# The interleaved MLP stages of a decoder trunk: from the scheduler's order to an order written in the source

## The chip, the cores and the metric

One core of a Trainium2 chip runs the whole program. The metric is the device time of one execution in microseconds (us). The engines are TensorE (PE in the profile; its weight loads are PEld), VectorE (DVE), ScalarE (ACT), GpSimd (POOL) and SyncE (SP), which issues the weight transfers.

## The reference

A trunk of two layers over 256 tokens of width 2048, in float32. Each layer is a mixer (MLA beside mLSTM in the first, dilated window attention in the second) and then an MLP; a final norm follows. The change touches the MLPs alone:

```python
def squared_relu_mlp(h, w1, w2):
    return jnp.square(jax.nn.relu(h @ w1)) @ w2     # w1: 2048 x 8192, w2: 8192 x 2048

x = x + squared_relu_mlp(rms_norm(x, norm_mlp[layer]), mlp_w1[layer], mlp_w2[layer])
```

## The kernel before, in words

**Splitting.** Every weight tile comes by one 512 KB transfer on SP's queue into one of four raw buffers (`load`, L118) and is split into two float32r halves (`halves`, L130): ScalarE copies it to "hi" (L135), then VectorE subtracts to get "lo" (L136). Four hi and four lo buffers serve the ordinary splits. A product is three matmuls: hi by hi, hi by lo, lo by hi (`mm_three`, L152).

**First matrix.** The hidden width of 8192 is done in four quarters (NQ) of 16 blocks of 128 columns. A block (`blocks`, L1089, by `steps_feats`, L265) takes two weight tiles; for each, `mm_feats` (L158) issues 8 matmuls of 512 columns (L164, operands T and wh) and 8 of 256 (L168, wl). It accumulates in the PSUM bank of `acc(..., 3)`, L95: each of the four "acc" banks is one buffer. After the second tile `evac_h` (L1031) empties it: ScalarE copies it out (bt_h, L1037), VectorE adds the two halves (hu, L1039), ScalarE applies ReLU and the square. For two blocks at a time of the first 12 of a quarter (SEVEN = 6 pairs), VectorE then forms differences in hp (L1053 to L1055) and the result pt is split (L1057, L1058); each of the last four blocks is split as it is (ht, L301 and L302).

**Second matrix.** Per quarter and per half of the output columns (c = 0 and 1024), `steps_seven` (L193) does 6 pairs of block rows by a seven-product scheme and the last two pairs plainly. A pair has two steps. `go_a` loads two raw tiles r0 and r1, forms the sums ta and tb on VectorE (L224 to L226), splits r0, half of r1, ta and tb, and issues three products (9 matmuls) into the "ym" tiles m1, m5, m7. `go_b` issues four products (12 matmuls): one into m6, three into the accumulators "yc" in banks 0, 1 and 2, in the order (1,0), (0,1), (0,0). The four ym tiles take the other four PSUM banks. A plain step (`eight`, L248) has one weight tile and 12 matmuls into yc; the second of them opens the fourth accumulator (1,1) in bank 3.

**Emptying.** After the last pair `early_y` (L1063) uses m1, m5, m6, m7: one ScalarE copy and eight VectorE operations, four of which add into x (L1067). After the last plain step `late_y` (L1082) adds the four yc tiles into x (L1086), in the order (1,1), (1,0), (0,1), (0,0).

**Order.** A stage is one quarter's half of the output columns, interleaved with the 8 blocks of the first matrix that are next: with c = 0 blocks 8 to 15 of the same quarter, with c = 1024 blocks 0 to 7 of the next. `woven` (L444) puts one or two steps of the pairs ahead of each block: a b block, a block, b a block, b block, and so on, with a block last; then come the four plain steps. A layer has seven such stages, then a last part on its own. Within the order that the source gives, the framework's scheduler decides at compile time how the instructions stand in each engine's queue. Each queue is worked through in its order.

Of the kernel before, what the change touches and what calls it, by code (L numbers as in the profile page):

```python
# [14 lines left out]
P = 128  # L15
# [54 lines left out]
def trunk(ctx: ExitStack, tc: tile.TileContext, plan, a, c_first, c_even, c_odd, out):  # L70
# [122 lines left out]
    def steps_seven(pool, H, pairs, w, c, early, late, name="y", hold=()):  # L193
# [12 lines left out]
        def seven(k):  # L206
            first, last = k == pairs[0], k == pairs[-1]
            end = last and not rest
            t = {}

            def product(ac, i, h, l, j, last):
                pt = H[2 * k][0]
                mm_three(ac, (pt[:, 0, i, :], pt[:, 1, i, :]), (h[:, j, :], l[:, j, :]), first, last)

            def go_a():
                if first:
                    box["m"] = {i: mis(f"{name}m{i}") for i in (1, 5, 7, 6)}
# [43 lines left out]
            return go  # L261

        return [seven(k) for k in pairs], [[eight(k, j) for j in range(2)] for k in rest]

    def steps_feats(Ts, w, c0, evac, n=256, name="f", kt=4, bank=None):  # L265

# [757 lines left out]
    def mlp(layer, norm, nxt):  # L1024
        st = ExitStack()
        sm = st.enter_context(tc.tile_pool(name=f"mlp{layer}", bufs=1))
        X = Late(norm.T)
        scale = {}
        NF = FF // NQ // P

        def evac_h(H):  # L1031
            def make(c):
                box = {}

                def go(f, ac):
                    t = sm.tile([P, 512], F32, name="bt_h", tag="bt", bufs=2)
                    nc.scalar.activation(t, ac, AF.Copy)  # L1037
                    u = sm.tile([P, S], F32, name="hu", tag="hu", bufs=2)
                    nc.vector.tensor_add(u, t[:, :S], t[:, S:])  # L1039
                    nc.scalar.activation(u, u, AF.Relu)  # L1040
                    if c >= SEVEN:
                        nc.scalar.activation(u, u, AF.Square)
                        H[2 * c + f] = sm.tile([P, 2, S], FR, name="ht", tag="ht", bufs=2 * (NF // 2 - SEVEN))
                        split_to(H[2 * c + f], u)
# [5 lines left out]
                    v = u.rearrange("p (b t) -> p b t", b=NB)  # L1050
                    nc.scalar.activation(dst, v, AF.Square)
                    if f == 1:
                        nc.vector.tensor_tensor(r[:, 4:6, :], r[:, 1:3, :], r[:, 2:4, :], OP.subtract)  # L1053
                        nc.vector.tensor_tensor(r[:, 6, :], r[:, 5, :], r[:, 1, :], OP.subtract)
                        nc.vector.tensor_tensor(r[:, 7, :], r[:, 0, :], r[:, 6, :], OP.add)  # L1055
                        pt = sm.tile([P, 2, 8, P], FR, name="pt", tag="pt", bufs=SEVEN)
                        nc.scalar.activation(pt[:, 0], r, AF.Copy)  # L1057
                        nc.vector.tensor_tensor(pt[:, 1], r, pt[:, 0].bitcast(F32), OP.subtract)  # L1058
                        H[2 * c], H[2 * c + 1] = (pt, 0), (pt, 1)
                return go  # L1060
            return make

        def early_y(c):  # L1063
            def go(m1, m5, m6, m7):
                def add(b, j, src):
                    v = x[b][c + j]
                    nc.vector.scalar_tensor_tensor(v, src, scale["s"][:, b:b + 1], v, OP.mult, OP.add)  # L1067

                p = sm.tile([P, 512], F32, name="yp", tag="yp", bufs=1)
                q = sm.tile([P, 512], F32, name="yq", tag="yq", bufs=1)  # L1070
                nc.scalar.activation(p, m1, AF.Copy)
                add(0, 0, m1)
                nc.vector.tensor_add(p, m6, p)
                nc.vector.tensor_add(q, m7, p)
                nc.vector.tensor_sub(p, m5, p)
                add(1, 0, q)
                nc.vector.tensor_sub(q, m5, q)
                add(0, 1, p)
                add(1, 1, q)
            return go  # L1080

        def late_y(c):  # L1082
            def go(cc):
                for b, j in ((1, 1), (1, 0), (0, 1), (0, 0)):
                    v = x[b][c + j]
                    nc.vector.scalar_tensor_tensor(v, cc[b, j], scale["s"][:, b:b + 1], v, OP.mult, OP.add)  # L1086
            return go

        def blocks(q, H):  # L1089

            ev = evac_h(H)

            def block(i):
                def go():
                    run(steps_feats(X, ("mlp_w1", layer, 0), q * (FF // NQ) + i * P,
                                    lambda f, ac: ev[i // 2](i % 2, ac), n=P, name="h", kt=8, bank=3))
                return go

            ev = [ev(c) for c in range(NF // 2)]
            return [block(i) for i in range(NF)], ev  # L1100

        H = [None] * NF
        hs, ev = blocks(0, H)
        steps = steps_feats(X, ("mlp_w1", layer, 0), 0, ev[0], name="h")
        run(steps[:3])
        norm.turn(3)
        run(steps[3:])
        norm.close()
        scale["s"] = norm.inv_var()
        for c in range(1, NF // 4):  # L1110
            run(steps_feats(X, ("mlp_w1", layer, 0), c * 256, ev[c], name="h"))
        for q in range(NQ):
            last = q == NQ - 1
            wq = ("mlp_w2", layer, q * (FF // NQ))
            seven, eight = steps_seven(sm, H, list(range(SEVEN)), wq, 0, early_y(0), late_y(0))
            woven(hs[NF // 2:], sum(seven, []))
            run(*eight)
            if last and nxt is None:
                finish(H, wq, early_y(2), scale, sm)
                break  # L1120
            pairs = list(range(3 if last else SEVEN))
            seven, eight = steps_seven(sm, H, pairs, wq, 1024, early_y(2), late_y(2))
            if last:
                nxt.stats(0)
                nxt.stats(1)
                steps = sum([a + b for a, b in zip(seven, eight)] + eight[len(seven):], [])
                run(steps[:-1], [lambda: nxt.turn(0)], steps[-1:], [lambda: nxt.turn(1)])
                break
            H = [None] * NF
            hs, _ = blocks(q + 1, H)  # L1130
            sv = sum(seven, [])
            woven(hs[:NF // 2], sv)
            run(*eight)
        if nxt is not None:
            nxt.stats(2)
            nxt.stats(3)
        return st
# [63 lines left out]
```

## Time and profile before

| | us |
|---|---|
| runs (3), median | 2117.52 |
| lowest, highest | 2115.13, 2119.45 |
| profiled execution, its time | 2115.02 |
| profiled execution, its span | 2113.2 |

The span is from the first to the last instruction in the trace. In rows of a timeline the first number is the start in us, the second the duration; ends of matmuls are modelled, so how long one takes in a sequence is read from start to start. "Idle before" names what the engine waited for.

### The profile page before, as it was taken

To read this page: it belongs to the slowest core of one execution; us is meant where nothing else is said; L and a number is where in the kernel's file an instruction comes from. 1 tells how busy PE (TensorE), PEld (TensorE's weight loads), DVE (VectorE), ACT (ScalarE), POOL (GpSimd) and SP (SyncE) were. 2 spreads that over 40 slices of the span, in tenths; PEclk is the share of its full clock that TensorE was granted. 3 is DMA by queue.
4 is the path that set the end of the run, shared out by engine and by line. 5 is a ranking of instruction groups with operands and counts; after the bars stand their busy time and mean duration, and the time that the engine had idled before them with its cause. 6 is when DMAs were issued, how large, how long until landed. Compare 5 with 4: busy or idle time off the path is not lost.

```text
span 2113.2 us, 29343 instructions
## 1 busy us (share of the span) xinstructions
PE 2093.8 (99%) x10860; PEld 1797.8 (85%) x10860; DVE 1742.3 (82%) x2455; ACT 1303.7 (62%) x1876; POOL 6.1 (0%) x13
## 2 busy tenths in 40 slices
PE   9999999999999999999999999999999999999998
PEld 8998888888888888888888888888888888888886
DVE  5678555889999999999877667568899998999998
ACT  6575445766676666667544444457666666667665
POOL 0000000000000000000000000000000000000000
PEclk9999999999999999999999999999999999999999
DMA  8554455556565566566665555455565665656664
GB/s 295 165 174 158 160 176 187 178 191 216 183 211 197 190 202 204 192 205 195 197 194 174 170 179 170 163 186 178 193 205 194 206 201 188 204 194 200 203 213 162
DMA packets 115296, 404.51 MB, mean 191 GB/s; under 512 B 12944, under 2 KB 13584, under 8 KB 115152
## 3 DMA queue, kind: packets, MB, share of 16 engines
q1 hardware_dynamic: 114048, 400.02, 57.9%
q8 instruction: 85, 1.39, 0.3%
q0 software_dynamic: 384, 1.51, 0.2%
q10 hardware_dynamic: 720, 1.11, 0.1%
q14 instruction: 59, 0.48, 0.1%
HBM read 400.49 MB, written 2.10 MB: 191 GB/s over the span
## 4 chain that ended last, share of the span: by engine, by line
PE 88%; DVE 7%; DMA 2%; issue 1%; ACT 1%; SPq 0%; POOLq 0%; POOL 0%; DVEq 0%; ACTq 0%
PE h L164 21%; PE h L168 11%; PE yc L155 4%; PE yc L156 4%; PE yc L154 4%; PE ym L155 4%; PE ym L156 3%; PE ym L154 3%; DVE wl L136 3%; PE k L164 3%; PE o L154 3%; PE o L156 3%; PE o L155 3%; PE q L164 3%; PE v L154 2%; PE v L156 2%
## 5 line engine op out<-in xcount | busy, mean ns | idle before, releaser
L136 DVE TENSOR_TENSOR wl<-wr,wh 128x1024 fp32r<-128x1024 f32 (+4 forms) x769 | 865.6, 1134 | 259.8 <-ACT wh L135 254.5
L135 ACT ACTIVATE wh<-wr 128x1024 fp32r<-128x1024 f32 (+4 forms) x769 | 753.8, 986 | 515.6 <-PE h L164 136.6
L164 PE MATMUL h<-T,wh 128*128 128x512 f32 x2048 | 511.4, 392 | 1.1 <-ACT wh L135 0.9
L164 PEld LDWEIGHTS h<-T,wh 128*128 128x128 f32 x2048 | 374.5, 188 | 76.0 <-ACT wh L135 2.6
L168 PEld LDWEIGHTS h<-T,wl 128*128 128x128 f32 x2048 | 279.3, 190 | 20.1
L168 PE MATMUL h<-T,wl 128*128 128x256 f32 x2048 | 285.5, 282 | 0.0
L155 PE MATMUL ym<-wl,pt 128*128 128x512 f32 x360 | 142.2, 395 | 1.8 <-DVE wl L136 1.8
L154 PE MATMUL ym<-wh,pt 128*128 128x512 f32 x360 | 140.1, 394 | 0.2 <-ACT wh L135 0.2
L156 PE MATMUL ym<-wh,pt 128*128 128x512 f32 x360 | 140.2, 389 | 0.0
L224 DVE TENSOR_TENSOR ta<-wr,wr 128x1024 f32<-128x1024 f32 x90 | 110.1, 1223 | 33.1 <-DMA wr<-in_mlp_w 32.4
L135 ACT ACTIVATE wh<-ta 128x1024 fp32r<-128x1024 f32 x90 | 95.2, 1058 | 61.0 <-DVE ta L224 60.9
L155 PE MATMUL yc<-wl,pt 128*128 128x512 f32 x318 | 124.0, 390 | 0.0
L154 PE MATMUL yc<-wh,pt 128*128 128x512 f32 x318 | 123.2, 390 | 0.0
L156 PE MATMUL yc<-wh,pt 128*128 128x512 f32 x318 | 122.8, 389 | 0.0
L1040 ACT ACTIVATE hu<-hu 128x256 f32<-128x256 f32 x128 | 52.6, 415 | 99.5 <-DVE hu L1039 99.3
L135 ACT ACTIVATE wh<-tb 128x1024 fp32r<-128x1024 f32 x90 | 94.7, 1052 | 28.5 <-DVE tb L226 28.3
L136 DVE TENSOR_TENSOR wl<-tb,wh 128x1024 fp32r<-128x1024 f32 x90 | 109.7, 1219 | 1.9 <-ACT wh L135 1.7
L136 DVE TENSOR_TENSOR wl<-ta,wh 128x1024 fp32r<-128x1024 f32 x90 | 109.7, 1219 | 0.0
L154 PE MATMUL o<-wh,M 128*128 128x512 f32 x256 | 102.3, 399 | 0.0
L156 PE MATMUL o<-wh,M 128*128 128x512 f32 x256 | 99.8, 390 | 0.0
L155 PE MATMUL o<-wl,M 128*128 128x512 f32 x256 | 99.7, 389 | 0.0
L154 PE MATMUL yc<-wh,ht 128*128 128x512 f32 (+1 forms) x256 | 99.4, 388 | 0.0
(297 smaller groups left out, 3320.9 us busy)
## 6 DMA issues: line engine op xcount, KB each, us to landing
wr<-in_mlp_w SPq DMA_DIRECT2D x512, 512.0 KB, 4.1
wr<-in_od_w_qkv SPq DMA_DIRECT2D x96, 512.0 KB, 4.1
wr<-in_ev_w_in SPq DMA_DIRECT2D x32, 512.0 KB, 3.5
wr<-in_ev_w_out SPq DMA_DIRECT2D x32, 512.0 KB, 3.4
wr<-in_od_w_out SPq DMA_DIRECT2D x32, 512.0 KB, 3.5
wr<-in_ev_w_in SPq DMA_DIRECT2D x24, 344.0 KB, 3.1
wr<-in_ev_w_in SPq DMA_DIRECT2D x15, 364.0 KB, 5.8
wr<-in_mla_w_ukv SPq DMA_DIRECT2D x8, 512.0 KB, 3.7
```

Source lines behind the costliest of these rows:

```text
L135: nc.scalar.activation(hi, raw, AF.Copy)
L136: nc.vector.tensor_tensor(lo, raw, hi.bitcast(F32), OP.subtract)
L154: nc.tensor.matmul(ac, xh, hi, start=first, stop=False)
L155: nc.tensor.matmul(ac, xh, lo, start=False, stop=False)
L156: nc.tensor.matmul(ac, xl, hi, start=False, stop=last)
L164: nc.tensor.matmul(acs[f], hi[:, j, f * P:(f + 1) * P], Ts[j].rearrange("p a t -> p (a t)"), start=first and j == 0, stop=False)
L168: nc.tensor.matmul(acs[f][:, :S], lo[:, j, f * P:(f + 1) * P], Ts[j][:, 0, :], start=False, stop=last and j == n - 1)
L224: nc.vector.tensor_tensor(ta, r0, r1[:, 0:1, :].to_broadcast([P, 2, 512]), OP.add)
L1040: nc.scalar.activation(u, u, AF.Relu)
```

## The change

`drive` takes a list of units and writes out, for ScalarE, VectorE and TensorE, the very order in which they work (`manual_schedule`). A unit has its splits and sums (`prep`), its matmuls (`go`) and the kinds of buffers that it frees. At step n, `drive` first emits what is due "now", then splits for coming units, as far as buffers of the kinds w (4), t (3) and q (1) are left, alternating with the other work that is due; the first split that finds no buffer stops those behind it. Then come unit n's matmuls. What these return (copies, additions) is due one to four units later. Each stage's order is the pattern, with "s" for a pair (two units) and "h" for a block (two units), and then the four plain units. All 14 stages are in two such lists, one per layer. The half tile of r1 gets buffers of its own (q); ta has one buffer instead of two; the late additions come as (1,0), (0,1), (0,0), (1,1).

```diff
-                ta = pool.tile([P, 2, 512], F32, name=f"ta{n_w[0]}", tag="ta", bufs=2)
+                ta = pool.tile([P, 2, 512], F32, name=f"ta{n_w[0]}", tag="ta", bufs=1)
...
+    def drive(units, left):
+        ahead = [(n, kind, f) for n, u in enumerate(units) for kind, f in u.prep]
+        due = {}
+        for n, u in enumerate(units):
+            first, rest = due.pop(n, ([], []))
+            splits = []
+            while ahead and left.get(ahead[0][1], 1) > 0:
+                _, kind, f = ahead.pop(0)
+                if kind:
+                    left[kind] -= 1
+                splits.append(f)
+            assert not ahead or ahead[0][0] > n
+            run(first, [f for pair in zip(splits, rest) for f in pair], splits[len(rest):], rest[len(splits):])
+            for d, now, f in u.go() or ():
+                due.setdefault(n + d, ([], []))[not now].append(f)
+            for kind in u.free:
+                left[kind] += 1
...
+            return [Unit([(None, sums), ("w", split(0, lambda: t["r0"])), ("t", split(1, lambda: t["ta"], pool, "t", 3))],
+                         go_a, ["t"]),
+                    Unit([("q", split(3, lambda: t["r1"][:, 1:2, :], pool, "q", 1)),
+                          ("t", split(2, lambda: t["tb"], pool, "t", 3))], go_b, ["w", "q", "t"])]
...
+                due = [(1, True, copy), (1, False, add), (2, False, square)]
+                if c >= SEVEN:
+                    return due + [(3, False, plain)]
+                return due + ([(3, False, sums), (4, False, pair)] if f == 1 else [])
...
+                return [(1, True, both(nc.scalar.activation, p, m1, AF.Copy)),
+                        (1, True, add(0, 0, m1)),
+                        (1, False, both(nc.vector.tensor_add, p, m6, p)),
+                        (1, False, both(nc.vector.tensor_add, q, m7, p)),
+                        (2, False, both(nc.vector.tensor_sub, p, m5, p)),
+                        (2, False, add(1, 0, q)),
+                        (3, False, both(nc.vector.tensor_sub, q, m5, q)),
+                        (3, False, add(0, 1, p)),
+                        (4, False, add(1, 1, q))]
...
+                return [(1, True, add(b, j)) for b, j in ((1, 0), (0, 1), (0, 0), (1, 1))]
...
+                    if g == 0:
+                        box["a"] = acc("h", 3)
+                    mm_feats([box["a"]], [X[k] for k in range(8 * g, 8 * g + 8)], *t["w"], g == 0, g == 1)
+                    if g == 1:
+                        return ev(i, box["a"])
...
+        pattern = "shshhshhshhshs"
+        units = []
         for q in range(NQ):
...
+                for what in pattern:
+                    units += (seven if what == "s" else hs).pop(0)
+                units += eight
...
+        with tc.manual_schedule(engines={mybir.EngineType.PE, mybir.EngineType.Activation, mybir.EngineType.DVE}):
+            drive(units, {"w": 4, "t": 3, "q": 1})
```

## Rows read from the trace of the kernel before

**Rows 1.** The page, part 1: busy time of each engine over the span.

```profile
PE 2093.8 (99%) x10860; PEld 1797.8 (85%) x10860; DVE 1742.3 (82%) x2455; ACT 1303.7 (62%) x1876; POOL 6.1 (0%) x13
```

**Rows 2.** Busy times by stretch, the interleaved parts; columns PE, PEld, DVE, ACT, POOL, clock, DMA.

```profile
400.00:1000.00 600.00, 598.42 (x3048) 509.22 (x3047) 558.25 (x680) 400.80 (x537) 0.00 (x0) 1.00 0.61 198
1470.00:2050.00 580.00, 578.43 (x2948) 491.12 (x2947) 537.97 (x658) 387.21 (x515) 1.12 (x2) 1.00 0.61 199
```

**Rows 3.** The timeline of TensorE, one block of the first matrix: start, duration.

```profile
407.20 1.98 PE L164 MATMUL h<-T,wh 128*128 128x512 f32 x8
409.01 1.11 PE L168 MATMUL h<-T,wl 128*128 128x256 f32 x8
409.96 2.00 PE L164 MATMUL h<-T,wh 128*128 128x512 f32 x8
411.81 1.12 PE L168 MATMUL h<-T,wl 128*128 128x256 f32 x8
412.76 0.40 PE L154 MATMUL ym<-wh,pt 128*128 128x512 f32 x1
```

**Rows 4.** Groups of TensorE's matmuls between 400 and 1000 us: count, busy, mean.

```profile
L164 PE MATMUL h<-T,wh 128*128 128x512 f32 x904 | 225.0, 391 | 0.5 <-ACT wh L135 0.5
L168 PE MATMUL h<-T,wl 128*128 128x256 f32 x904 | 126.0, 282 | 0.0
```

**Rows 5.** The timeline at the end of a block: two matmuls in flow, the next unit, the copy.

```profile
606.68 0.62 PE L164 MATMUL h<-T,wh 128*128 128x512 f32 x2
...
608.09 0.40 PE L154 MATMUL ym<-wh,pt 128*128 128x512 f32 x1
...
608.30 0.58 ACT L1037 ACTIVATE bt_h<-h 128x512 f32<-128x512 f32 x1
```

**Rows 6.** The timeline where TensorE waited for a block's copy.

```profile
1820.90 0.58 ACT L1037 ACTIVATE bt_h<-h 128x512 f32<-128x512 f32 x1
...
1821.53 0.73 PE L164 MATMUL h<-T,wh 128*128 128x512 f32 x2 [0.15 <-ACT bt_h L1037]
```

**Rows 7.** The timeline of VectorE in the plain steps at a stage's end.

```profile
480.88 1.23 DVE L224 TENSOR_TENSOR ta<-wr,wr 128x1024 f32<-128x1024 f32 x1
482.02 0.69 DVE L136 TENSOR_TENSOR wl<-wr,wh 128x512 fp32r<-128x512 f32 x1
482.62 0.69 DVE L225 TENSOR_TENSOR tb<-ta,wr 128x512 f32<-128x512 f32 x1
483.23 1.23 DVE L136 TENSOR_TENSOR wl<-ta,wh 128x1024 fp32r<-128x1024 f32 x1
484.37 1.41 DVE L1086 SCALAR_TENSOR_TENSOR x<-yc,iv_mlp,x 128x512 f32<-128x512 f32 x2
485.69 0.68 DVE L226 TENSOR_TENSOR tb<-tb,wr 128x512 f32<-128x512 f32 x1
```

**Rows 8.** Groups of ScalarE between 400 and 1000 us: the split's first half.

```profile
L135 ACT ACTIVATE wh<-wr 128x1024 fp32r<-128x1024 f32 x185 | 194.3, 1055 | 83.3 <-PE h L164 57.8 <-PE yc L156 13.2 <-issue 7.4
```

**Rows 9.** Busy times from 470 to 504 us, across a stage's end; columns as above.

```profile
470.00:504.00 34.00, 34.00 (x172) 28.92 (x171) 33.58 (x41) 21.04 (x28) 0.00 (x0) 1.00 0.58 201
```

**Rows 10.** VectorE's waits between 400 and 1000 us: total, times, longest.

```profile
DVE ta L224 <- DMA wr<-in_mlp_w: 13.0, 18, 1.6
```

**Rows 11.** Busy times of the last 9 us; columns as above.

```profile
2104.00:2113.00 9.00, 0.95 (x8) 0.75 (x7) 3.31 (x11) 2.78 (x8) 0.56 (x1) 0.66 0.55 202
```

**Rows 12.** The timeline of TensorE at the start of the program.

```profile
4.44 0.98 PE L154 MATMUL c<-wh,T 128*128 128x364 f32 x2 [4.44 <-ACT wh L135]
...
10.35 0.51 PE L155 MATMUL c<-wl,T 128*128 128x364 f32 x1
10.65 0.51 PE L156 MATMUL c<-wh,T 128*128 128x364 f32 x1
...
11.22 0.33 PE L155 MATMUL c<-wl,T 128*128 128x364 f32 x1
11.39 0.33 PE L156 MATMUL c<-wh,T 128*128 128x364 f32 x1
```

More of the change, by code (lines that the diff above doesn't have):

```diff
@@ new lines, in units_seven, with seven, product, sums @@
+    def units_seven(pool, H, pairs, w, c, early, late, name="y"):
+        box = {}
+        rest = [k for k in range(len(H) // 2) if k not in pairs]
+        def seven(k):
+            first, last = k == pairs[0], k == pairs[-1]
+            t = {}
+            def product(ac, i, h, l, j, last):
+                pt = H[2 * k][0]
+                mm_three(ac, (pt[:, 0, i, :], pt[:, 1, i, :]), (h[:, j, :], l[:, j, :]), first, last)
+            def sums():
+                t["r0"] = r0 = load(w, [(2 * k, c, 512), (2 * k + 1, c + 512, 512)], (2, 512))
+                t["r1"] = r1 = load(w, [(2 * k, c + 512, 512), (2 * k + 1, c, 512)], (2, 512))
+                n_w[0] += 1
+                t["ta"] = ta = pool.tile([P, 2, 512], F32, name=f"ta{n_w[0]}", tag="ta", bufs=1)
+                t["tb"] = tb = pool.tile([P, 2, 512], F32, name=f"tb{n_w[0]}", tag="tb", bufs=1)
+                nc.vector.tensor_tensor(ta, r0, r1[:, 0:1, :].to_broadcast([P, 2, 512]), OP.add)
+                nc.vector.tensor_tensor(tb[:, 0, :], ta[:, 0, :], r0[:, 1, :], OP.add)
+                nc.vector.tensor_tensor(tb[:, 1, :], tb[:, 0, :], r1[:, 1, :], OP.add)
+            def split(to, src, *where):
+                def go():
+                    t[to] = halves(src(), *where)
+                return go
+            def go_a():
+                if first:
+                    box["m"] = {i: mis(f"{name}m{i}") for i in (1, 5, 7, 6)}
+                m = box["m"]
+                product(m[1], 1, *t[0], 0, last)
+                product(m[5], 5, *t[1], 0, last)
+                product(m[7], 4, *t[1], 1, last)
+            def go_b():
+                if first:
+                    box["c"] = {i: acc(f"{name}c{i[0]}{i[1]}", n) for n, i in enumerate(((1, 0), (0, 1), (0, 0)))}
+                m, cc = box["m"], box["c"]
+                end = last and not rest
+                product(m[6], 6, *t[2], 0, last)
+                product(cc[1, 0], 3, *t[2], 1, end)
+                product(cc[0, 1], 7, *t[0], 1, end)
+                product(cc[0, 0], 0, *t[3], 0, end)
+                if last:
+                    return early(m[1], m[5], m[6], m[7])
+            return [Unit([(None, sums), ("w", split(0, lambda: t["r0"])), ("t", split(1, lambda: t["ta"], pool, "t", 3))],
+                         go_a, ["t"]),
+                    Unit([("q", split(3, lambda: t["r1"][:, 1:2, :], pool, "q", 1)),
+                          ("t", split(2, lambda: t["tb"], pool, "t", 3))], go_b, ["w", "q", "t"])]
+        def eight(k, j):
+            t = {}
+            def split():
+                t["w"] = weights(w, 2 * k, 2, c + 512 * j, 512)
+            def go():
+                cc = box["c"]
+                if k == rest[0] and j == 1:
+                    cc[1, 1] = acc(f"{name}c11", 3)
+                hi, lo = t["w"]
+                for i in range(2):
+                    for b in range(NB):
+                        mm_three(cc[b, j], operand(H[2 * k + i], b), (hi[:, i, :], lo[:, i, :]),
+                                 (b, j) == (1, 1) and k == rest[0] and i == 0, k == rest[-1] and i == 1)
+                if k == rest[-1] and j == 1:
+                    return late(cc)
+            return Unit([("w", split)], go, ["w"])
+        return [seven(k) for k in pairs], [eight(k, j) for k in rest for j in range(2)]
@@ L1091, in blocks, with at_once, units_h, unit @@
+            return due
+        def at_once(f):
+            return lambda *arg: run([go for _, _, go in f(*arg)])
+        w1 = ("mlp_w1", layer, 0)
+        def units_h(q, H, blocks):
             ev = evac_h(H)
-            def block(i):
+            def unit(i, g, box):
+                t = {}
+                def split():
+                    t["w"] = weights(w1, 8 * g, 8, q * (FF // NQ) + i * P, P)
                 def go():
-                    run(steps_feats(X, ("mlp_w1", layer, 0), q * (FF // NQ) + i * P,
-                                    lambda f, ac: ev[i // 2](i % 2, ac), n=P, name="h", kt=8, bank=3))
-                return go
@@ L1099, in blocks @@
-            ev = [ev(c) for c in range(NF // 2)]
-            return [block(i) for i in range(NF)], ev
+                    if g == 0:
[3 more added lines that the diff above has]
+                        return ev(i, box["a"])
+                return Unit([("w", split)], go, ["w"])
+            out = []
+            for i in blocks:
+                box = {}
+                out.append([unit(i, g, box) for g in range(2)])
@@ L1102, in mlp, with evac @@
+            return out
         H = [None] * NF
-        hs, ev = blocks(0, H)
-        steps = steps_feats(X, ("mlp_w1", layer, 0), 0, ev[0], name="h")
+        ev = evac_h(H)
+        def evac(c):
+            return lambda f, ac: run([go for _, _, go in ev(2 * c + f, ac)])
+        steps = steps_feats(X, w1, 0, evac(0), name="h")
         run(steps[:3])
@@ L1110, in mlp @@
         for c in range(1, NF // 4):
-            run(steps_feats(X, ("mlp_w1", layer, 0), c * 256, ev[c], name="h"))
+            run(steps_feats(X, w1, c * 256, evac(c), name="h"))
+        pattern = "shshhshhshhshs"
+        units = []
         for q in range(NQ):
-            last = q == NQ - 1
             wq = ("mlp_w2", layer, q * (FF // NQ))
-            seven, eight = steps_seven(sm, H, list(range(SEVEN)), wq, 0, early_y(0), late_y(0))
-            woven(hs[NF // 2:], sum(seven, []))
-            run(*eight)
@@ L1118, in mlp @@
[L1118 to L1133, printed above, removed]
+            G = [None] * NF
+            for c, hs in ((0, units_h(q, H, range(NF // 2, NF))), (1024, units_h(q + 1, G, range(NF // 2)))):
+                if q == NQ - 1 and c > 0:
+                    break
+                seven, eight = units_seven(sm, H, list(range(SEVEN)), wq, c, early_y(c // 512), late_y(c // 512))
+                for what in pattern:
+                    units += (seven if what == "s" else hs).pop(0)
+                units += eight
@@ new lines, in mlp @@
+            if q < NQ - 1:
+                H = G
+        with tc.manual_schedule(engines={mybir.EngineType.PE, mybir.EngineType.Activation, mybir.EngineType.DVE}):
+            drive(units, {"w": 4, "t": 3, "q": 1})
+        early, late = at_once(early_y(2)), at_once(late_y(2))
+        if nxt is None:
+            finish(H, wq, early, scale, sm)
+        else:
+            seven, eight = steps_seven(sm, H, list(range(3)), wq, 1024, early, late)
+            nxt.stats(0)
+            nxt.stats(1)
+            steps = sum([a + b for a, b in zip(seven, eight)] + eight[len(seven):], [])
+            run(steps[:-1], [lambda: nxt.turn(0)], steps[-1:], [lambda: nxt.turn(1)])
```

83 lines of the change are left out of this document (44 added, 39 removed).

## The prediction, made before the changed kernel ran

> **What bounds the kernel now.** I read the busy times first [rows 1], then the two long stretches that the change rewrites [rows 2], then TensorE's own timeline in them. TensorE is busy 99% of the span; in the interleaved stretches 598.4 of 600 us and 578.4 of 580 us. VectorE stands next with 558 and 538 us, 93%. The busy time of matmuls says little of headroom, so I look at starts: eight 512-column matmuls take 1.81 us, 0.227 us each, eight 256-column ones 0.95 us, 0.119 us each, and one block's two halves of the first matrix follow each other in 2.76 and 2.80 us with no hole [rows 3]. With the counts [rows 2, 4] the first stretch needs at least 904 x (0.227 + 0.119) + 1240 x 0.227 = 594 us of its 600. So 6 us in 600 is all that any order can win there; with the second stretch, 12 us in all. That is the cap on the gain.
>
> The Trainium skill (Perfetto Trace Analysis, "Identifying the Most-Contended Engine") judges TensorE's headroom by the share of weight loads instead; with 85% here that would leave up to 15% of these 1180 us, some 177 us, to a better order. The trace does not bear that out: back-to-back matmuls start every 0.227 us while the loads are 85% busy, so that free share is no hole.
>
> **The change, part by part.** Names: a pair of the seven-product scheme is units A (9 matmuls, 2.04 us) and B (12, 2.72 us); a block of the first matrix is two units h (8 x 0.227 + 8 x 0.119 = 2.77 us each); a plain unit is E (12 matmuls, 2.72 us). A stage is 6 pairs, 8 blocks, then four E. Each layer has 7 stages in the list, 14 in all. Number of matmuls, loads, splits and additions: the same. SP still issues one load per raw tile in the order of use; r1 is now kept until its split can have the single "q" buffer. "ta" goes to one buffer; in order, its readers are done before the next pair's sum, so I take 0 for it, with 0 to 1 us for each of the six pairs that stay outside the list.
>
> 1. *Blocks that follow each other.* Before, every block had a pair's unit behind it. The new pattern s h s hh s hh s hh s h s has three places per stage, 42 in all, where a block directly follows a block. Both accumulate in bank 3, which has one buffer; so TensorE has to wait until ScalarE has copied the first block out. The price is in the trace: the next matmul after a block started at 608.09, the block's copy at 608.30, 0.21 us later, and took 0.58 [rows 5]. Where TensorE did wait for such a copy, it went on at 1821.53, 0.05 us after the copy's end, and its first two matmuls then took 0.73 us [rows 6] where two in full flow take 0.62 [rows 5], 0.11 more. Sum 0.21 + 0.58 + 0.05 + 0.11 = 0.95 us. The change puts the copy first in its step, so nothing else should stand before it on ScalarE. Bounds: 0.84 (no slow restart, 35 us in all) and about 1.3 (ScalarE still has a 0.4 us remainder of the last step, where it waited for VectorE; 55 us). I take 0.95: 42 x 0.95 = 40 us.
>
> 2. *The end of a stage on VectorE.* Start to start, VectorE takes 1.14 us for a 128x1024 operation, 0.60 for a 128x512 one, 0.66 for an addition into x [rows 7]. A split waits for its slot to be freed by TensorE and for ScalarE's half, about 1.06 us [rows 8]. The order in the last steps: at the last B, all four "w" slots are taken (the last pair's and three E's), so the fourth E's split heads the line and everything after it waits; VectorE has nothing to do in that step. From the last B's end on it is fed everything at once. Counted from there, after a stage of blocks 0 to 7: 0.27 until ScalarE's half is there; the fourth E's split 1.14; the differences of a block (512 columns in three operations) 0.73, an estimate; the next pair's sums 1.14 + 0.60 + 0.60; two early additions 1.32. Next step: split of A 1.14, the block's own split 1.14, ta's 1.14, early 0.66, q 0.60, early 0.66, tb's 1.14. Next: 1.14, 0.66, 0.66. Next: 1.14, 0.66, and the sums of the pair after, 2.34. Only then, in the step after the last E, come the late additions: the first, which frees bank 0, ends at 19.6 us. TensorE gets to the matmul that writes bank 0 after four E, A and three matmuls: 10.9 + 2.04 + 0.68 = 13.6 us. It stands still for 6.0 us (partly sooner, at the bank that the early additions still read; that is in it). After a stage of blocks 8 to 15 one split and the differences fall away and a split of 256 columns comes in, 0.30 as half of the 512-column one, an estimate: 18.0, so 4.4 us. Six such ends lie inside each layer's list, three of each kind: 2 x 3 x (6.0 + 4.4) = 62 us. Bounds: 0, since the old order runs VectorE at 33.6 of 34 us across such an end and TensorE at 34 of 34 [rows 9], and 62 plus 12 waits of 0.7 for a raw tile, as VectorE's sums met 18 times in 600 us [rows 10], 71 us. I take 62, as the order is written out and VectorE's work adds up in it.
>
> Why the old order had no such hole: there a block stood behind the last pair, so the early additions had 5.5 us more of matmuls beside them, and the late additions stood ahead of the next stage's sums.
>
> 3. *What goes away.* The present holes, up to 12 us; I counted the new ones from zero, so all 12 come off.
>
> Sum against the profiled execution: 2115.0 + 40 + 62 - 12 = 2205 us. It ran 2.5 us under the median of the runs, 2117.5; on that footing the forecast is **2208 us**.
>
> **The rivals.**
> *VectorE keeps up* (0.20). Only the 42 copies cost: 2117.5 + 40 - 12 = 2145 us. For it: the same work went by without a hole before [rows 9]. Against it: the order puts 18 us of work ahead of the late additions. It decides if VectorE enters the four E with its queue empty and some 5 us of it done earlier.
>
> *The clock falls in the new holes* (0.15). TensorE's granted clock: in the stretches of [rows 2] it is 1.00; in the last 9 us, where TensorE was busy for 0.95 us only, it is 0.66 [rows 11]. At the start, on the lower level, matmuls of 364 columns began 0.30 us apart, from 4.44 us to about 11; then 0.17 [rows 12]. If each stage's hole brought the clock down to 1.2 GHz for as long as it lasted at the start, 6.7 us of which half is lost, that is 12 x 3.4 = 41 us more: 2249 us. Against it: no hole before was like these, and each is broken by A's matmuls. The Trainium skill (TensorE: Matmul & The Clock Gate, Part 1) has the clock halved after idleness, which speaks for this rival; no run so far shows holes of this kind.
>
> *Faster* (0.03). If a block that follows a block cost nothing and VectorE kept up, the 12 us come off: 2105 us. For this the place to look is bank 3: the wait would have to be under 12/42 = 0.29 us, while the copy alone takes 0.58. Only a second accumulator would do it, and the diff gives bank 3 for every block.
>
> *It doesn't do what it says* (0.03): TensorE's order comes out as before and nothing moves: 2117 us. Against: the pattern differs in the source itself.
>
> **How the numbers follow.** The forecast has 0.59; its own range, with the bounds of terms 1 and 2 (35 to 55 and about 40 to 71), is 2180 to 2235. The range that should hold 8 in 10 takes in most of "VectorE keeps up" and half of the clock: 2138 to 2248. A measurement of this kernel can tell about 0.2%, 4 us, from no change. Faster by over that 0.04, within it 0.02, slower 0.94.
>
> **What would show it.** Right: in a stage, waits of TensorE's "h" matmuls for the bt_h copy, 42 times about 0.8 us; waits of "yc" matmuls for the late additions to x and of "ym" for the early ones, together 4 to 6 us at each of 12 places; VectorE without a gap there and idle in the last B before them; the rest at 0.227 us per matmul. VectorE's share of the stretch falls to about 87%. Wrong: if TensorE doesn't wait for bt_h, term 1 falls; if the late additions end before TensorE wants bank 0, term 2 falls; if the granted clock is under 1 after the holes, the clock rival holds; waits of "ym" for weight splits in mid-stage would be a cause that I left out.

## The result and the profile after

The changed kernel takes 2345.03 us (median of 4 runs, 2342.42 to 2351.77) against 2117.99 of the kernel before: ratio 1.108, 95% interval 1.105 to 1.111. That is 227 us slower; 2208 were forecast, with a range to 2248. It got slower, as forecast, but by far more, and the time lies outside the range. The profiled execution took 2343.45 us with a span of 2341.6.

The page of the changed kernel, busy times and the clock in 40 slices, and its stretch from 420 to 980 us by busy times (columns as in [rows 2]):

```profile
PE 2166.0 (92%) x10860; PEld 1843.2 (79%) x10860; DVE 1763.6 (75%) x2455; ACT 1298.8 (55%) x1876; POOL 6.2 (0%) x13
...
PEclk9999999999999899999999999999999999999999
```

```profile
420.00:980.00 560.00, 494.48 (x2387) 415.87 (x2386) 442.39 (x526) 309.39 (x413) 0.00 (x0) 0.94 0.52 166
```

Against [rows 1] the counts of instructions are the same and VectorE's busy time has hardly grown; in the stretch every engine is less busy than in [rows 2], TensorE 88% instead of 99.7%, VectorE 79% instead of 93%. And the granted clock is 0.94, where it was 1.00. The page's slices round that away: only one shows an 8.

What TensorE waited for, by the profile's waits (total, times, longest), the three longest:

```profile
PE h L164 <- ACT bt_h L1146: 83.9, 42, 2.8
PE yc L154 <- DVE x L1215: 56.1, 12, 4.7
PE ym L154 <- DVE yq L1198: 16.5, 12, 2.5
```

Before, the three rows were 0.2 us or absent. The counts are those of the prediction: 42 blocks behind a block, 12 stage ends. To see all that TensorE loses, also to the clock, I go by starts ("by starts" below too): for each matmul of the MLPs, the time from its start to the next one's, less 0.227 us (512 columns) or 0.119 to 0.120 (256). The sums, by what stands at the hole:

| | before | changed |
|---|---|---|
| a block waits for the last block's copy (bank 3) | 0 | 90.6 |
| a pair's matmul waits (ym and yc, nearly all at a stage's end) | 0.4 | 77.1 |
| matmuls at the lower clock | 0 | 58.7 |
| restarts after a wait, and other | 8.1 | 8.7 |
| sum | 8.5 | 235.1 |

The difference, 226.6 us, is the whole of the result. The 42 waits are not alike: in every stage the first is about 0.85 us, the second and third 2.3 or 3.0. One of the long ones, in rows from the timeline of all engines at a block that follows a block (start, duration):

```profile
534.97 1.23 DVE L1179 TENSOR_TENSOR pt<-hp,pt 128x1024 fp32r<-128x1024 f32 x1 [0.85 <-ACT pt L1178]
...
536.29 0.42 ACT L1163 ACTIVATE hp<-hu 128x256 f32<-128x256 f32 x1 [1.05 <-DVE pt L1179]
...
536.62 2.00 ACT L135 ACTIVATE wh<-wr 128x1024 fp32r<-128x1024 f32 x2
...
537.69 1.23 DVE L136 TENSOR_TENSOR wl<-wr,wh 128x1024 fp32r<-128x1024 f32 x1 [1.50 <-ACT wh L135]
...
538.84 1.22 DVE L314 TENSOR_TENSOR ta<-wr,wr 128x1024 f32<-128x1024 f32 x1
539.19 1.11 PE L168 MATMUL h<-T,wl 128*128 128x256 f32 x8
...
540.09 1.06 ACT L135 ACTIVATE wh<-ta 128x1024 fp32r<-128x1024 f32 x1 [1.48 <-DVE ta L314]
...
541.57 1.04 ACT L135 ACTIVATE wh<-tb 128x1024 fp32r<-128x1024 f32 x1
542.52 0.58 ACT L1146 ACTIVATE bt_h<-h 128x512 f32<-128x512 f32 x1
...
543.14 2.11 PE L164 MATMUL h<-T,wh 128*128 128x512 f32 x8 [2.85 <-ACT bt_h L1146]
```

Read it backwards. TensorE ends the block at about 540.1 and goes on at 543.14, as soon as the copy of 542.52 is done. The copy is first in its step, but ScalarE is still in the step before: it makes the halves of ta and tb, for which it waited on VectorE's sums. VectorE had begun those late since it waited 1.50 us for ScalarE's half of a split; and ScalarE was late with that because its write to hp had to wait for VectorE's split of the old one. Two queues in a fixed order hand a delay to and fro, and each wait in it is on the other engine. Ahead of the first such copy of a stage the same kinds of split are listed; there ScalarE is through with them as the block ends (at 523.2 us in the next stage), and the wait is 0.85 us.

A stage's end, TensorE's and VectorE's timelines:

```profile
496.86 0.39 PE L156 MATMUL ym<-wh,pt 128*128 128x512 f32 x1
497.71 0.47 PE L154 MATMUL ym<-wh,pt 128*128 128x512 f32 x1 [0.46 <-DVE yq L1198]
...
498.25 0.40 PE L156 MATMUL ym<-wh,pt 128*128 128x512 f32 x1
503.33 0.79 PE L154 MATMUL yc<-wh,pt 128*128 128x512 f32 x1 [4.68 <-DVE x L1215]
503.92 0.63 PE L155 MATMUL yc<-wl,pt 128*128 128x512 f32 x1
504.35 0.63 PE L156 MATMUL yc<-wh,pt 128*128 128x512 f32 x1
```

```profile
484.14 0.75 DVE L1195 SCALAR_TENSOR_TENSOR x<-ym,iv_mlp,x 128x512 f32<-128x512 f32 x1 [1.42 <-ACT yp L1198]
...
498.14 1.21 DVE L136 TENSOR_TENSOR wl<-wr,wh 128x1024 fp32r<-128x1024 f32 x1
499.28 0.74 DVE L1195 SCALAR_TENSOR_TENSOR x<-yq,iv_mlp,x 128x512 f32<-128x512 f32 x1
499.94 1.22 DVE L314 TENSOR_TENSOR ta<-wr,wr 128x1024 f32<-128x1024 f32 x1
501.19 0.69 DVE L315 TENSOR_TENSOR tb<-ta,wr 128x512 f32<-128x512 f32 x1
501.92 0.69 DVE L316 TENSOR_TENSOR tb<-tb,wr 128x512 f32<-128x512 f32 x1
502.53 2.72 DVE L1215 SCALAR_TENSOR_TENSOR x<-yc,iv_mlp,x 128x512 f32<-128x512 f32 x4
```

This is the prediction's second term in the order that it wrote down: split, early addition, the sums of the pair after, and only then the late additions, for whose first bank 0 waits. After the wait the matmuls begin 0.43 us apart instead of 0.227. The same place by stretches, columns as before:

```profile
495.00:503.30 8.30, 3.19 (x13) 2.00 (x12) 8.23 (x11) 2.12 (x2) 0.00 (x0) 0.83 0.57 190
503.30:507.30 4.00, 3.97 (x9) 3.14 (x10) 4.00 (x5) 0.00 (x0) 0.00 (x0) 0.50 0.02 4
507.30:512.90 5.60, 5.60 (x33) 4.91 (x32) 4.40 (x5) 3.48 (x4) 0.00 (x0) 1.00 0.62 193
```

In the first stretch TensorE is idle for 5 of 8.3 us and the clock falls; in the second the clock is at half, 1.2 GHz, while TensorE works without a hole; then it is full again.

### The profile page after: what moved, and what is told of

Its sections match the earlier page's. It is cut to its first block, busy times and chain, and to the rows that moved or that the text cites. A ratio compares the mean times of both kernels' runs of the same rounds, so it can differ in the third digit from the quotient of the medians.

```text
span 2341.6 us, 29238 instructions
## 1 busy us (share of the span) xinstructions
PE 2166.0 (92%) x10860; PEld 1843.2 (79%) x10860; DVE 1763.6 (75%) x2455; ACT 1298.8 (55%) x1876; POOL 6.2 (0%) x13
## 4 chain that ended last, share of the span: by engine, by line
PE 68%; DVE 17%; ACT 9%; issue 5%; DMA 2%; SPq 0%; DVEq 0%; POOLq 0%; POOL 0%; ACTq 0%
PE h L164 17%; PE h L168 8%; DVE wl L136 7%; ACT wh L135 6%; DVE ta L314 3%; PE yc L154 3%; PE k L164 3%; PE o L154 2%; PE o L156 2%; PE o L155 2%; PE q L164 2%; PE yc L155 2%; PE yc L156 2%; PE v L154 2%; PE v L156 2%
## 5 line engine op out<-in xcount | busy, mean ns | idle before, releaser
L164 PE MATMUL h<-T,wh 128*128 128x512 f32 x2048 | 542.3, 409 | 83.9 <-ACT bt_h L1146 83.9
L164 PEld LDWEIGHTS h<-T,wh 128*128 128x128 f32 x2048 | 390.2, 198 | 168.9 <-ACT bt_h L1146 92.4
L168 PEld LDWEIGHTS h<-T,wl 128*128 128x128 f32 x2048 | 291.7, 198 | 22.2
L168 PE MATMUL h<-T,wl 128*128 128x256 f32 x2048 | 296.5, 289 | 0.0
L154 PE MATMUL yc<-wh,pt 128*128 128x512 f32 x318 | 133.3, 423 | 56.2 <-DVE x L1215 56.1
L154 PE MATMUL ym<-wh,pt 128*128 128x512 f32 x360 | 141.3, 396 | 17.3 <-DVE yq L1198 16.5
L1146 ACT ACTIVATE bt_h<-h 128x512 f32<-128x512 f32 x128 | 74.9, 591 | 119.0 <-PE h L168 118.6
L155 PE MATMUL yc<-wl,pt 128*128 128x512 f32 x318 | 131.9, 415 | 0.2
L156 PE MATMUL yc<-wh,pt 128*128 128x512 f32 x318 | 131.2, 413 | 0.0
L154 PEld LDWEIGHTS yc<-wh,pt 128*128 128x128 f32 x318 | 64.2, 202 | 76.0 <-DVE x L1215 62.8
L314 DVE TENSOR_TENSOR ta<-wr,wr 128x1024 f32<-128x1024 f32 x84 | 102.3, 1218 | 4.1 <-DVE wl L136 2.2
L155 PE MATMUL yc<-wl,ht 128*128 128x512 f32 (+1 forms) x256 | 99.3, 388 | 0.4 <-DVE wl L136 0.4
L155 PE MATMUL o<-wl,M 128*128 128x512 f32 x256 | 99.7, 389 | 0.0
```

Source lines behind the costliest of these rows:

```text
L154: nc.tensor.matmul(ac, xh, hi, start=first, stop=False)
L155: nc.tensor.matmul(ac, xh, lo, start=False, stop=False)
L156: nc.tensor.matmul(ac, xl, hi, start=False, stop=last)
L164: nc.tensor.matmul(acs[f], hi[:, j, f * P:(f + 1) * P], Ts[j].rearrange("p a t -> p (a t)"), start=first and j == 0, stop=False)
L168: nc.tensor.matmul(acs[f][:, :S], lo[:, j, f * P:(f + 1) * P], Ts[j][:, 0, :], start=False, stop=last and j == n - 1)
L1146: nc.scalar.activation(box["t"], ac, AF.Copy)
```

## The experiments

Each is the changed kernel with one edit, unless it says otherwise; all ran beside the kernel before, at 2115 to 2118 us.

**e1, the order left to the scheduler.**

```diff
-        with tc.manual_schedule(engines={mybir.EngineType.PE, mybir.EngineType.Activation, mybir.EngineType.DVE}):
+        if True:
             drive(units, {"w": 4, "t": 3, "q": 1})
```

> The changed kernel's units and lists, but ScalarE's, VectorE's and TensorE's order left to the scheduler. Theory (the holes come from blocks that share bank 3 back to back and from VectorE's work listed ahead of the late additions): the scheduler can put copies and late additions earlier, so the stage-end holes (77 us in the changed kernel) and most of the long bank-3 holes go; 42 bank-3 waits of about 0.95 us may stay: 2115 to 2165 us. Rival 1 (the sequence of units in the source is what costs, fixed or not): 2300 us or more. Rival 2 (fixing the order is itself the whole cost): within 5 us of 2118.

Measured: 2149.39 us, ratio 1.016 (1.014 to 1.017). Nearly 200 us of the 227 go with the fixed order. The scheduler does more than I thought: it moves TensorE's units too, so that no block follows a block (never more than 32 matmuls of a block in a row, in the stretch from 420 to 1040 us), and the bank-3 waits are all gone. What it leaves is the stage's end, where the last pair still stands right before the plain units, with 12 waits for the late additions:

```profile
PE yc L154 <- DVE x L1215: 18.3, 12, 2.5
```

**e2, the sequence of units of the kernel before, order fixed.** The pattern names units, "a b h a h b a h ..." as `woven` gave them.

```diff
-        pattern = "shshhshhshhshs"
+        pattern = "abhahbahbhabhahbahbh"
...
+                halves_of = sum(seven, [])
...
-                    units += (seven if what == "s" else hs).pop(0)
+                    units += hs.pop(0) if what == "h" else [halves_of.pop(0)]
```

> The changed kernel with the order fixed as there, but the units in the sequence of the kernel before: one or two units of a pair ahead of each block, a block last. Theory: no block follows a block, and the last block stands between the early additions and the plain units, so no wait for bank 3, no clock below 1 and stage-end holes under 1 us: 2105 to 2130 us. Rival (fixing the order is the whole cost, whatever the sequence): over 2250 us.

Measured: 2231.98 us (1.055, 1.054 to 1.057). Theory and rival both miss. No block follows a block, yet the waits are there in other places, here by the profile's waits of TensorE:

```profile
PE yc L154 <- DVE x L1215: 35.4, 6, 5.9
PE yc L154 <- ACT ht L406: 23.6, 7, 3.9
PE h L164 <- ACT bt_h L1146: 19.4, 14, 2.2
PE yc L156 <- DVE ht L407: 10.1, 6, 1.8
```

After a stage of blocks 0 to 7 the late additions are still 5.9 us late; after one of blocks 8 to 15 the plain units wait for the last block's own split (ht), which `drive` lists three units after the block. And at 14 places even a block behind a pair's unit waits for the copy, since ScalarE is late with it. So a fixed order has to suit the sequence in every queue; this one doesn't suit the old sequence either. The last block does cover the early additions, as I had claimed: no wait for yq is left. It doesn't cover the late ones, which are still listed behind the sums of two coming pairs, nor its own split.

**e3, no block behind a block, the last pair still at the end** (pattern `abhahbhahbhahbhahbab`).

> Fixed order; the pattern changed so that no block follows a block, while the last pair still stands right before the plain units. Theory: the bank-3 waits (91 us) and the slow clock after them (33 us) go, the stage-end holes (77 us) and the slow clock after those (25 us) stay: about 2215 us, 2195 to 2235. Rival (one cause, VectorE short of time everywhere, so that holes move and don't go): 2300 us or more.

Measured: 2255.23 us (1.066, 1.065 to 1.068), 20 us above the expected span. The bank-3 waits went, 91 us, and the cost of the lower clock fell by 31. But waits ahead of a pair's matmuls grew from 77 to 110 us: the early additions' from 16.5 to 27.5, and new ones for weight splits:

```profile
PE yc L154 <- DVE x L1215: 53.0, 14, 4.7
PE ym L154 <- DVE yq L1198: 27.5, 12, 2.8
PE ym L155 <- DVE wl L136: 13.1, 18, 1.1
```

**e4, ScalarE free for the copy.** In the last step before a block that follows a block, no splits are listed.

```diff
-            while ahead and left.get(ahead[0][1], 1) > 0:
+            nxt = units[n + 1] if n + 1 < len(units) else None
+            quiet = getattr(u, "tail", False) and nxt is not None and getattr(nxt, "head", False)
+            while not quiet and ahead and left.get(ahead[0][1], 1) > 0:
...
+                u.head, u.tail = g == 0, g == 1
```

> The changed kernel, but in the step before a block that follows a block no splits are listed, so that ScalarE has nothing to do ahead of the copy; they come one step later. Theory (the second and third bank-3 waits of a stage, 2.3 and 3.0 us, are ScalarE's queue: splits that wait for VectorE stand ahead of the copy): all 42 waits come to 0.85 us, 36 us instead of 91, and the clock stays up after them (33 us): about 2257 us, 2245 to 2280. Rival (the copy itself or TensorE's restart is slow there): 2335 to 2355 us.

Measured: 2297.15 us (1.086, 1.084 to 1.087). The mechanism is as stated: all 42 waits are 0.85 us by starts, 35.5 us together, and no slow clock stands behind them. TensorE's waits for the copy and for the late additions, and a stretch with three waits for the copy and one other hole, of 0.74 us:

```profile
PE h L164 <- ACT bt_h L1148: 28.8, 42, 0.7
PE yc L154 <- DVE x L1217: 52.6, 18, 4.7
```

```profile
510.00:586.00 76.00, 73.36 (x375) 62.03 (x374) 59.35 (x73) 46.97 (x65) 0.00 (x0) 1.00 0.55 180
```

The time fell by 48 us instead of 88, since the waits ahead of a pair's matmuls grew here too, from 77 to 112 us. Of that growth of 35 us, 21 are in the waits for the early additions (18 to 39), and at one stage's end the traces show why. The first plain matmul, and VectorE's last addition of two halves of a block (hu) before the early additions, in the changed kernel and then in e4:

```profile
484.17 0.39 PE L154 MATMUL yc<-wh,ht 128*128 128x512 f32 x1
482.31 0.42 DVE L1151 TENSOR_TENSOR hu<-bt_h 128x256 f32<-128x256 f32 x1
```

```profile
479.64 0.39 PE L154 MATMUL yc<-wh,ht 128*128 128x512 f32 x1
480.09 0.42 DVE L1153 TENSOR_TENSOR hu<-bt_h 128x256 f32<-128x256 f32 x1
```

From hu to the end of the early work that TensorE waits for (yq), VectorE takes 15.3 us in both. But TensorE, with its bank-3 waits shortened, is there 4.5 us sooner and VectorE only 2.2, so TensorE waits 2.3 us more for yq. What a shorter wait gives back is partly lost again at the stage's end. The other 16 us are waits for weight splits in the units around it.

**e5 and e6, one side of the order fixed:** `engines={PE}` in e5, `engines={Activation, DVE}` in e6.

> The changed kernel, with TensorE's order alone fixed; ScalarE's and VectorE's are left to the scheduler. Theory (VectorE has almost no time to spare, 41 us idle of 560 in the kernel before against 118 in the changed one, and the fixed order of ScalarE and VectorE makes it idle): VectorE's idle time falls to about 50 of 560, the 42 bank-3 waits stay at 0.85 to 1 us, stage-end holes shrink to 2 us or less each, the clock stays up: 2140 to 2185 us. Rival (TensorE's own fixed order is what costs): 2250 us or more.

> The changed kernel, with ScalarE's and VectorE's order fixed and TensorE's left to the scheduler. Theory: VectorE goes on idling, so TensorE's holes stay at the stage ends, and blocks that follow each other may be moved apart: 2220 to 2345 us. Rival (TensorE's fixed order is the cost): 2175 us or less.

Measured: e5 2226.52 us (1.051, 1.049 to 1.053), e6 2321.73 us (1.097, 1.095 to 1.099). Either side alone costs. With TensorE's order fixed the 42 waits stay, 61 us of them, as the first in each stage is 1.4 to 4.7 us (the others 0.85), and the scheduler can't take them apart. With ScalarE's and VectorE's order fixed TensorE goes without the bank-3 waits, but waits for the weights of units that it now takes out of the order of the splits:

```profile
PE ym L154 <- ACT wh L135: 104.6, 83, 3.7
```

e5 misses its theory by 40 us and lies under its rival. e6 is inside its theory's span, but by luck: of the holes at the stage's end that the theory kept, the early additions' 19 us by starts are there, the late additions' are gone, and the waits for weights, which it didn't have, fill the span.

**e7, as e4, and the late additions sooner:** besides, no splits and sums are listed in the last two plain units of a stage.

```diff
+            u.quiet = k == rest[-1]
```

> As the run in which the copies find ScalarE free, and besides no splits or sums are listed in the last two plain units of a stage, so that the late additions stand sooner in VectorE's order. Theory of the prediction (the hole is the work listed ahead of the late additions): those waits, 56 us in that run, fall under 15 us, the early ones stay near 55, the slow clock halves: about 2240 us, 2215 to 2260. Rival (VectorE is short of time, the holes move to the weight splits of the next units): 2280 us or more.

Measured: 2232.12 us (1.054, 1.052 to 1.056), inside the theory's span. The wait for the late additions, by starts 56 us in e4, is 13 us, and the lower clock costs 16 us instead of 28:

```profile
PE yc L154 <- DVE x L1219: 11.0, 18, 1.0
```

The other waits ahead of a pair's matmuls, which the theory had staying near 55 us, fell too, from 56 to 42. So the late additions, two thirds of the 65 us that e7 gains on e4, bear out the second term of the prediction: the hole is work listed ahead of them.

**e8, VectorE's half of a split listed one item later.**

> The changed kernel, but VectorE's half of each split is listed after the next item of the step instead of right behind ScalarE's half, so that VectorE has other work while ScalarE makes its half. Theory (a good part of VectorE's idle time is the wait for ScalarE's half of a split whose slot has just come free): VectorE's wait for ScalarE's halves, 90 us of 560, falls by a third or more, and the time to 2250 to 2310 us. Rival (the idle time comes from the steps in which nothing can be split): 2330 us or more.

Measured: 2353.43 us (1.111, 1.109 to 1.113). VectorE's waits for ScalarE's halves fall from 89.7 us (of 560) to 76.7 only, and TensorE's waits don't shrink: for bank 3 they come to 88.2 us by the profile (83.9 in the changed kernel), for the late additions to 68.2 (56.1). That theory falls; to move VectorE's half by itself gains nothing.

**e9, the old sequence, no order fixed.**

> The changed kernel's lists with the units in the sequence of the kernel before and no order fixed: with the runs so far the fourth corner of sequence (old, new) by order (free, fixed). Theory (both cost: the fixed order lets VectorE idle, the new sequence puts blocks back to back and the last pair at the end): 2113 to 2128 us. Rival (something else of the change costs, the lists' lookahead or the one ta buffer): 2140 us or more.

Measured: 2121.32 us (1.003, 1.002 to 1.004). With it there are four corners:

| | order free | order fixed |
|---|---|---|
| old sequence | 2121 | 2232 |
| new sequence | 2149 | 2345 |

Fixing costs 111 us in the old sequence and 196 in the new; the new sequence costs 28 us free and 113 fixed. All else of the lists costs about 6 us (e9 against its kernel before, 2115.5).

**e10, e15 and e16, small edits of the change in the kernel before.** e15: the half of r1 split into buffers of its own and one ta buffer; e16: the late additions' new order; e10: both.

```diff
-                t[3] = halves(r1[:, 1:2, :])
+                t[3] = halves(r1[:, 1:2, :], pool, "q", 1)
```

> The kernel before with three small edits of the change alone: the half tile of r1 in buffers of its own, one ta buffer, the late additions in the order (1,0), (0,1), (0,0), (1,1). Theory (these are not what costs; at most the 12 us of present holes can be won): 2108 to 2122 us. Rival (one ta buffer delays VectorE's sums): 2130 us or more.

> The kernel before with the half tile of r1 in buffers of its own and one ta buffer, late additions as before. If the own buffers make the gain of 5 us: 2109 to 2113 us. If the order of the late additions does: 2115 to 2119.

> The kernel before with the late additions in the order (1,0), (0,1), (0,0), (1,1) alone. If that order makes the gain: 2109 to 2113 us; if the buffers do: 2115 to 2119.

Measured: e10 2110.74 us (0.998, 0.997 to 0.999), e15 2110.49 us (0.997, 0.996 to 0.998), e16 2115.73 us (1.000, 0.999 to 1.001). The buffers make the gain of 5 to 6 us, the order of the late additions none. e10 and e15 are faster than both kernels. In e15 the long waits for a raw tile [rows 10] are nearly gone between 400 and 1000 us:

```profile
DVE ta L224 <- DMA wr<-in_mlp_w: 1.9, 7, 0.5
```

That the separate buffers free the raw tiles sooner is my reading of this row; it wasn't tried by itself.

**e11, the differences of the blocks on GpSimd,** otherwise as e7.

> As the run with free copies and late additions listed sooner (2232 us), but the three differences of each pair of blocks are done by GpSimd, which is idle; that takes about 0.73 us from VectorE 42 times, 31 us in all. Theory (VectorE is the wall in the fixed order: what it is spared comes off the time): 2195 to 2225 us. Rival (the rest of the holes is waiting in a chain, not VectorE's load): 2230 us or more, and more still if GpSimd is slow or takes VectorE's port.

Measured: 2231.65 us (1.055, 1.053 to 1.056), no gain over e7. It doesn't decide between theory and rival: GpSimd needs 1.06 to 1.32 us for each of the three (medians; VectorE 0.29 to 0.42), the split behind them waits for it, and beside it VectorE's splits of 128x1024 take 1.29 us in the mean instead of 1.22. The group on GpSimd in e11, of the whole span, and then the group of splits in e7 and in e11, between 420 and 980 us:

```profile
L1175 POOL TENSOR_TENSOR hp<-hp 128x256 f32<-128x256 f32 x48 | 61.1, 1274 | 1815.5 <-ACT hp L1167 1090.9 <-DVE wl L136 724.7
```

```profile
L136 DVE TENSOR_TENSOR wl<-wr,wh 128x1024 fp32r<-128x1024 f32 x156 | 185.5, 1221 | 38.8 <-ACT wh L135 38.8
```

```profile
L136 DVE TENSOR_TENSOR wl<-wr,wh 128x1024 fp32r<-128x1024 f32 x158 | 198.6, 1288 | 36.0 <-ACT wh L135 35.9
```

**e12, the old sequence with TensorE's order alone fixed.**

> The old sequence of units with TensorE's order alone fixed. Theory: no bank-3 waits, ScalarE's and VectorE's order is the scheduler's: 2112 to 2130 us. Rival (TensorE's fixed order costs by itself, 84 us stayed when ScalarE and VectorE were free in the new sequence, and only part of that is bank 3): 2150 us or more.

Measured: 2155.00 us (1.019, 1.017 to 1.020), inside the rival's span. There are no long waits for bank 3; the plain units wait for the last block's split instead, 18.3 us at six places. So TensorE's fixed order costs some 34 us more than the free order of e9 even there. My reading is that the scheduler also uses TensorE's order to get round what is late: in e9, after a stage of blocks 8 to 15, TensorE takes a matmul of the next pair ahead of the last four plain ones; here all 48 plain ones come first.

**e13 and e14, more work for VectorE.** One of a pair's two additions into tb is done twice, 90 times 0.60 us, in e4 and in the kernel before.

```diff
                 nc.vector.tensor_tensor(tb[:, 1, :], tb[:, 0, :], r1[:, 1, :], OP.add)
+                nc.vector.tensor_tensor(tb[:, 1, :], tb[:, 0, :], r1[:, 1, :], OP.add)
```

> As the run in which the copies find ScalarE free (2297 us), with one 128x512 addition of each pair done twice on VectorE, 0.60 us 90 times, 84 of them in the lists; the result is the same. Theory (VectorE is short of time in the fixed order): 40 to 60 us more, 2337 to 2357. Rival (the holes are chains of waits, beside which VectorE has time): under 20 us more.

> The kernel before with the same addition done twice, 0.60 us 90 times, 54 us. VectorE idles 41 of 560 us there. If that idle time can be used: under 15 us more, 2118 to 2132. If VectorE is as good as full there too: 35 us more or above.

Measured: e13 2329.83 us (1.101, 1.099 to 1.102), 33 more than e4; e14 2140.94 us, 24 more than its kernel before (1.011, 1.010 to 1.013). Of 54 us of work 0.6 and 0.45 come through. Both lie between theory and rival: in either kernel about half of the added work costs time, and half runs beside waits. By starts, the waits for the early additions are 39 us in e13 as in e4; those for the late additions and for weight splits grew, and with them the cost of the clock. So the early waits that grew in e4 don't follow VectorE's load alone. What made them grow in e3, where the sequence of units differs too, stays open.

## Why the prediction was right and wrong

*What bounds the kernel, and the cap on the gain.* Right. The holes that could be won were put at 12 us; by starts they are 8.5, and the best version of the study gains 6.

*The sum.* The forecast had 90 us of loss, 227 were measured. Of the 137 us between, the lower clock is 59, for which the sum had nothing, term 1 is 51, term 2 is 15 and term 3 is 12.

*Term 1, blocks behind blocks: 42 x 0.95 = 40 us.* Place, count and mechanism right; the size failed. A wait with ScalarE free is 0.85 us and a restart of about 0.1, as worked out (e4: 35.5 us in 42 waits). But two of three were 2.3 or 3.0 us, and all 42 came to 91 us. The step that failed is "the change puts the copy first in its step, so nothing else should stand before it on ScalarE", with 0.4 us as the most that a remainder would add. First in its step isn't first in its queue: the step before still held four splits, two of them behind VectorE's sums. ("Every block had a pair's unit behind it" isn't quite so either: the last block of a stage had a plain one.)

*Term 2, the stage's end: 62 us.* Right in mechanism, low by a fifth: 77 us. The ends measured 5.5 and 7.3 us where 4.4 and 6.0 were worked out. The first late addition ends 19.1 and 20.9 us after the last B, where the sum had 18.0 and 19.6. About half of that is the first early addition, which the sum left out: it came only at the last B's end, as the first row of VectorE's timeline above shows, after 1.42 us of waiting for ScalarE's copy out of the same bank. The rest is the sums. A pair's sums were priced at 2.34 us, from rows where other work stands between them; in the changed kernel each has to wait for the one before, and they take 2.59 (499.94 to 502.53 above), twice. A block's three differences, estimated at 0.73, take 0.99. e7 took the listed work away and with it three quarters of the waits for the late additions.

*Term 3, the present holes: 12 us off.* They were 8.5 us, and nothing came off: restarts and other small holes cost 8.7 in the changed kernel.

*The rivals.* "VectorE keeps up", "faster" and "it doesn't do what it says" did not happen. "The clock falls" did, at 59 us: about 25 behind the stage ends, for which 41 were priced, and 34 behind the long bank-3 waits. This is the second step that failed, and the larger one: the forecast's sum had the matmuls after its own holes at full clock, and the rival got 0.15 beside the forecast's 0.59, as if one excluded the other. Put on top, with 40 + 62 + 41 - 12, the forecast would have been 2249, and with term 1 as measured 2300. (The rival's own 2249 is this sum; the forecast's own range, 2180 to 2235, comes to 2181 to 2232 by the bounds named there.) The rule of the Trainium skill that the prediction named (TensorE: Matmul & The Clock Gate, Part 1: the clock is halved after idleness) is borne out by the stretches above, 0.83, then 0.50, then 1.00.

*What would show it.* The signs came as listed: 42 waits for bt_h, 12 places of waits for early and late additions, and the granted clock under 1. VectorE's share fell to 79%, not 87%.

*Beyond the prediction.* I took the fixing itself for harmless and looked for the cost in the sequence alone. e1 and e9 show that the same lists cost 6 us in the old sequence and 34 in the new when the scheduler may reorder, and 117 and 227 when it may not (each against the kernel before in its own runs).

## What to carry to other kernels

Where two engines hand work to and fro in fixed order, price a step by the queue in front of it, not by its place in its step: ask what the instruction ahead of it waits for, and what that one waits for. Before fixing an order, look at what the free one reaches: here TensorE was 99.7% busy, so 8 us was all that any order could win, against 227 that it could lose. If a forecast has holes on TensorE, price the clock after them as part of the same case.

## What the runs showed of the hardware

The granted clock stayed at 1.00 through three waits of 0.85 us and a hole of 0.74 in 76 us of otherwise dense matmuls (e4). In the changed kernel it fell to half at each of the 12 waits of about 4.85 us, and after many, but not all, of those of 2.3 and 3.0 us. Two of these, alike in length, at 540 and at 559 us:

```profile
540.00:545.00 5.00, 2.15 (x11) 1.65 (x10) 4.93 (x7) 3.96 (x5) 0.00 (x0) 1.00 0.50 170
559.00:565.00 6.00, 3.16 (x10) 2.37 (x10) 5.93 (x8) 3.95 (x5) 0.00 (x0) 0.74 0.60 181
```

The clock (third number from the end) is full through the first and 0.74 on average at the second; what sets them apart stays open. A 512-column matmul at the lower level starts every 0.43 us. In all, the lower level cost 59 us of the 227.

In e11 the 118 of VectorE's 128x1024 splits that ran beside one of GpSimd's additions took 1.45 us in the mean, the other 688 took 1.22. One of GpSimd's own took 4.5 us, against a median of 1.06 for its group; the profile's spans on GpSimd are rough.
